# Thirty-two dense tokens of a retrieval layer take their U rows by gather; the dense U products go from 384 to 352 columns

## The chip, the core and the metric

The kernel runs on one core of a Trainium2 chip. The core has a matrix engine (TensorE, PE in the profile, with its weight loads as PEld), three elementwise engines (VectorE or DVE, ScalarE or ACT, GpSimd or POOL), a queue engine for transfers (SyncE, SP), 16 DMA engines, an on-chip memory of 128 partitions (SBUF) and accumulators (PSUM). The metric is the device time of one execution, in microseconds.

## The reference, cut to what matters

One encoder block for 512 tokens of width 1024: attention, a gated linear recurrence and their merge, and then the part that the change touches, a layer that retrieves 128 of 16384 one-neuron experts for each token (8 heads, 16 experts each):

```python
s, idx = lax.top_k(scores, K)                     # both halves of the keys, 128 each
cand = (s[:, :, 0, :, None] + s[:, :, 1, None, :]).reshape(T, PH, K * K)
cand_idx = (idx[:, :, 0, :, None] * PEER_NKEYS + idx[:, :, 1, None, :]).reshape(T, PH, K * K)
best, pos = lax.top_k(cand, K)
expert = jnp.take_along_axis(cand_idx, pos, axis=-1)
gate = jax.nn.softmax(best, axis=-1)
...
u = jnp.take(u_tab, eb, axis=0)                   # rows of U of the token's experts
a = jax.nn.gelu(jnp.einsum('td,thkd->thk', xb, u), approximate=False)
c = (a * gb).astype(h.dtype)
return jnp.einsum('thk,thkd->td', c, jnp.take(v_tab, eb, axis=0))
```

## The kernel before

The first 128 tokens (`GT`) are done by **gather**: for each of their 128 expert slots one indirect DMA on the POOL queue fetches 128 rows of a table that holds U and V side by side (1024 + 1024 numbers a row); DVE forms the dot product of the U half with the token (`rows<-rows,hrep`), ACT the activation and the gate (`gact`), and DVE adds the V half times that number to `gout`. The other 384 tokens (`ND`) are done **densely**: all 16384 experts are computed for all of them, and a matrix of gates that is zero almost everywhere picks out the right ones. The dense work goes by 128 blocks `e` of 128 experts:

- **U products** (`pieces`, `up`): for each block 8 slices of the width times 3 products (high and low parts of weights and activations, `whi`, `wlo`, `act_hi`, `act_lo`), 24 products of 128x128 weights with 384 columns. The weights are loaded (`raw<-in_u`, 3 buffers) and split by ACT (`whi`) and DVE (`wlo`). ACT's Gelu makes `gx` of the sum, and the result goes to DRAM (`gad`), or, for the last blocks (`fresh`), stays on the chip (`gf`).
- **Routing and spread** (`route`, `onehot`, `spread`): for 8 tokens `o` at a time DVE makes one-hot matrices of the two halves of the expert number (4 operations), PE multiplies them (16 products of 128 columns) into the 128x128 matrix of gates of each token, and ACT moves them to `gs`, which goes to DRAM as `gd`, 32 tokens at a time. There are 48 such steps. `fill` lets U products in between: it keeps a running sum of estimated PE time and of estimated DVE time, and issues the next slice of a U product as long as PE's sum is behind. A call `gathered(GO)` advances the gather by half a step for each `o`.
- **V stage** (`down`): for `n` = 0 to 127, in an order that mixes kept and fresh blocks, PE multiplies the weighted activations of a block with its rows of V: 3 blocks of 128 tokens, 2 halves of the width, 3 products of 512 columns, so 18 products. For that DVE weighs `ga` with the gates `gt` (`weigh`), and ACT and DVE split both operands (`chi`, `clo`, `vhi`, `vlo`). V comes by `vraw` (4 buffers), gates by `gt` (2 buffers of 4 blocks each), the kept activations by `ga` (5 buffers), all on SP's queue. The U products of fresh blocks stand between (`ups_due`), and the rest of the gather is spread evenly over the first 124 steps.

How many blocks are fresh is decided while the program is written: those that `fill` had not reached when the spread ended, less 8 (`LEAVE`) and a remainder that go before the V stage.

Of the kernel before, what the change touches and what calls it, by code (L numbers as in the profile page):

```python
# [41 lines left out]
G1, GO = 0.125, 0.5  # L42
# [10 lines left out]
ND = T - GT  # L53
GC = 0.125
# [40 lines left out]
def layout(x, positions, g_mix, w_in, g_q_lat, w_qb, g_kv_lat, w_kvb, w_a2, b_a2, g_gla, w_branch_a,  # L95
# [38 lines left out]
    a["u"] = ct(peer_u[0].reshape(128, 128, NC_D, 128).transpose(0, 3, 2, 1))  # L134
    a["uv"] = np.concatenate([peer_u[0], peer_v[0]], axis=1)
# [58 lines left out]
def body(ctx, tc, a, out):  # L194
# [209 lines left out]
    def proj(key, xs=None, bank="pmm"):  # L404
        w = weights(key)
        p = pmm(bank)
        acc(p if key[0] != "u" else p[:, GT:], pairs(w, NC_D), xs or hx)
        if key[0] != "u":
            further(key)
        return p  # L410
# [436 lines left out]
    h2d = [(hn[0][:, c, GT:], hn[1][:, c, GT:]) for c in range(NC_D)]  # L847

    def normed(c):
        q = tmp()  # L850
        dve.scalar_tensor_tensor(q[:, GT:], x2[:, c, GT:], cc(C_GFFN + c), r2[:, GT:], op0=OP.mult, op1=OP.mult)
        split(h2d[c][0], h2d[c][1], q[:, GT:], pool)
# [57 lines left out]
    aside = [columns_of] + [lambda i=i: rows_of(i) for i in range(2)] + [lambda i=i: plain_rows_of(i) for i in range(2)]  # L910
# [41 lines left out]
    gad = dr.tile([NB[0], 128, ND], F32, name="gad")  # L952

    def up_out(keep=0):

        while len(pend) > keep:
            e, p = pend.pop(0)
            if not place:
                g = tmp(n=ND)
            elif e < NB[0]:  # L960
                g = place[0].tile([128, ND], F32, name="gx", bufs=GX)
            else:
                g = ga[e] = dn.tile([128, ND], F32, name="gf", bufs=NF)
            act.activation(g, p[:, GT:], AF.Gelu)
            if e < NB[0]:
                act.dma_start(gad[e], g)
# [39 lines left out]
    sp.dma_start(gout, hd[1])  # L1006
# [3 lines left out]
    gsteps = [129]  # L1010

    def gather():

        rows = {}
# [38 lines left out]
    gd = dr.tile([128, T // TB, 128, TB], F32, name="gd")  # L1053
    GS = 2.0 ** 15
    def route(tt):
# [83 lines left out]
        if tt == 0:  # L1139
# [32 lines left out]
    def spread(o):  # L1172
# [44 lines left out]
    O0, NO = GT // 8, T // 8  # L1217
    for o in range(O0, NO + 1):
        if o < NO:
            if o == O0 or o % 16 == 0:  # L1220
# [3 lines left out]
                rate = 24.0 / (min(16, 16 - o % 16) - 1)  # L1224
            onehot(o)
# [7 lines left out]
        if o > O0:  # L1233
            spread(o - 1)
# [6 lines left out]
    EG = 4  # L1241
# [69 lines left out]
    def refill(queue=sp):  # L1311

        while made[0] < len(kept) and (made[0] < NA or kept[made[0] - NA] in used):
            e = kept[made[0]]
            ga[e] = dn.tile([128, ND], F32, name="ga", bufs=NA)
            queue.dma_start(ga[e], gad[e])
# [144 lines left out]
```

## Time and profile before

| | us |
|---|---|
| median of 3 runs (lowest to highest) | 1637.24 (1635.01 to 1640.02) |
| the profiled execution, its own time | 1637.02 |
| its span, from first to last instruction | 1635.2 |
| U, routing and spread, before the V stage (520 to 974 us) | 454 |
| V stage (974 to 1609 us) | 635 |

Read it as a list of stages: a stage is limited by its own engine or by transfers, and the mean over the span tells neither.

### The profile page before, as it was taken

Reading aid. Unit: us, or ns where it says so; the run is one execution under the profiler, and the core shown is the slowest. Engines: PE = TensorE matmul, PEld = TensorE weight load, DVE = VectorE, ACT = ScalarE, POOL = GpSimd, SP = SyncE. Lnnn points to the kernel's source line nnn. Section 1 sums busy time; section 2 is a strip of 40 time slices with the busy share of each in tenths; the row PEclk is TensorE's granted clock in tenths of the full one; section 3 lists DMA queues with packets and bytes.
Section 4 is the critical chain, followed back from the end, with each engine's and each line's share of the span. In section 5 each row is a group of like instructions: output and inputs, shape, how many; then the busy total and the mean of one; then the engine's idle time right before and its main releaser. Section 6 shows DMA issues by size and latency. Waiting matters only on the chain.

```text
span 1635.2 us, 23193 instructions
## 1 busy us (share of the span) xinstructions
PE 1603.7 (98%) x8487; PEld 1393.1 (85%) x8487; DVE 1240.3 (76%) x2517; ACT 726.0 (44%) x1252; POOL 355.6 (22%) x258
## 2 busy tenths in 40 slices
PE   7999999999999999999999999999999999999998
PEld 6777657888889999999999999888888888888876
DVE  6635665253897989889989747778988888988885
ACT  5453544243333646456455544344443443444343
POOL 4342243445354100000001111111211111111110
PEclk9999999999999999999999999999999999999999
DMA  5222122443333777788789898999999999999994
GB/s 172 64 89 78 52 71 91 169 146 110 125 115 111 233 264 279 261 311 296 266 311 348 330 345 296 318 361 347 392 383 350 386 365 370 367 344 361 364 379 152
DMA packets 154610, 415.82 MB, mean 254 GB/s; under 512 B 12343, under 2 KB 87608, under 8 KB 136448
## 3 DMA queue, kind: packets, MB, share of 16 engines
q1 hardware_dynamic: 118048, 230.28, 40.2%
q0 software_dynamic: 19888, 139.23, 22.2%
q10 hardware_dynamic: 16560, 44.83, 7.3%
q8 instruction: 66, 1.08, 0.3%
q14 instruction: 48, 0.39, 0.1%
HBM read 361.60 MB, written 52.17 MB: 253 GB/s over the span
## 4 chain that ended last, share of the span: by engine, by line
PE 83%; DMA 4%; DVE 4%; issue 4%; ACT 1%; POOL 1%; SPq 0%; DVEq 0%; POOLq 0%; ACTq 0%
PE pmm L161 61%; PE pst L161 11%; PE pk L161 10%; DMA ga<-gad 2%; DMA vraw<-in_v 1%; DVE vlo L161 1%; POOL wlo L242 1%; DMA raw<-in_u 1%; DVE rows L161 1%; DVE rB L161 0%; DVE gout L161 0%; ACT whi L236 0%; DVE tmp L161 0%; DVE clo L161 0%; DVE t L161 0%
## 5 line engine op out<-in xcount | busy, mean ns | idle before, releaser
L161 PE MATMUL pmm<-act_hi,whi 128*128 128x384 f32 (+1 forms) x1016 | 361.8, 356 | 9.4 <-ACT act_hi L331 9.0
L161 PE MATMUL pmm<-act_hi,wlo 128*128 128x384 f32 (+1 forms) x1016 | 353.5, 348 | 3.7 <-DVE wlo L161 2.0
L161 PE MATMUL pmm<-act_lo,whi 128*128 128x384 f32 (+1 forms) x1016 | 353.2, 348 | 0.5 <-DVE act_lo L161 0.5
L1019 POOL DMA_INDIRECT rows<-in_uv,gidx x128 | 130.8, 1022 | 890.5 <-DVE gout L161 846.7
L236 ACT ACTIVATE whi<-raw 128x1024 fp32r<-128x1024 f32 (+1 forms) x201 | 209.2, 1042 | 94.8 <-PE pmm L161 50.9
L242 POOL TENSOR_TENSOR wlo<-raw,whi 128x1024 fp32r<-128x1024 f32 (+1 forms) x79 | 186.2, 2361 | 250.2 <-ACT whi L236 211.5
L161 DVE TENSOR_TENSOR wlo<-raw,whi 128x1024 fp32r<-128x1024 f32 x122 | 148.9, 1223 | 91.4 <-ACT whi L236 89.8
L161 PEld LDWEIGHTS pmm<-act_hi,whi 128*128 128x128 f32 x1016 | 191.8, 189 | 23.8 <-ACT act_hi L331 9.0
L161 PEld LDWEIGHTS pmm<-act_hi,wlo 128*128 128x128 f32 x1016 | 191.6, 189 | 13.9 <-DVE wlo L161 2.6
L161 PE MATMUL pmm<-vlo,chi 128*128 128x512 f32 x512 | 200.5, 392 | 1.6 <-DVE vlo L161 1.3
L161 PE MATMUL pmm<-vhi,chi 128*128 128x512 f32 x512 | 199.6, 390 | 0.9 <-ACT vhi L1275 0.9
L161 PEld LDWEIGHTS pmm<-act_lo,whi 128*128 128x128 f32 x1016 | 192.0, 189 | 8.7 <-DVE act_lo L161 1.0
L161 PE MATMUL pmm<-vhi,clo 128*128 128x512 f32 x512 | 199.3, 389 | 0.0
L161 DVE SCALAR_TENSOR_TENSOR gout<-rows,gact,gout 128x1024 f32<-128x1024 f32 x128 | 164.4, 1284 | 0.0
L161 DVE TENSOR_TENSOR vlo<-vraw,vhi 128x1024 fp32r<-128x1024 f32 x128 | 156.4, 1222 | 4.7 <-ACT vhi L1275 4.7
L1275 ACT ACTIVATE vhi<-vraw 128x1024 fp32r<-128x1024 f32 x128 | 134.0, 1049 | 50.5 <-DMA vraw<-in_v 50.0
L161 DVE SCALAR_TENSOR_TENSOR rows<-rows,hrep 128x1024 f32<-128x1024 f32 x128 | 156.2, 1221 | 0.0
L161 PE MATMUL pmm<-t,whi 128*128 128x512 f32 x436 | 137.7, 397 | 0.0
L161 PEld LDWEIGHTS pmm<-vlo,chi 128*128 128x128 f32 x512 | 96.1, 188 | 25.7 <-DVE vlo L161 6.0
L1031 ACT ACTIVATE gact<-gact 128x1 f32<-128x1 f32 x128 | 25.8, 202 | 205.8 <-DVE rows L161 205.6
L161 PEld LDWEIGHTS pmm<-vhi,chi 128*128 128x128 f32 x512 | 96.1, 188 | 19.9 <-ACT vhi L1275 1.3
L161 PEld LDWEIGHTS pmm<-vhi,clo 128*128 128x128 f32 x512 | 96.1, 188 | 19.0
(276 smaller groups left out, 2775.3 us busy)
## 6 DMA issues: line engine op xcount, KB each, us to landing
raw<-in_u SPq DMA_DIRECT2D x128, 512.0 KB, 5.5
vraw<-in_v SPq DMA_DIRECT2D x124, 512.0 KB, 8.5
gt<-gd SPq DMA_DIRECT2D x30, 768.0 KB, 10.4
gd<-gs ACTq DMA_DIRECT2D x11, 2048.0 KB, 8.2
gad<-gx ACTq DMA_DIRECT2D x96, 192.0 KB, 5.0
ga<-gad SPq DMA_DIRECT2D x95, 192.0 KB, 9.6
raw<-in_w SPq DMA_DIRECT2D x28, 512.0 KB, 3.3
raw<-in_wpq SPq DMA_DIRECT2D x16, 512.0 KB, 3.5
```

What stands on the lines that cost most here:

```text
L161: return f(*args, **kw)
L236: act.activation(hi[:, :n], raw[:, :n], AF.Copy)
L242: (lo_eng or lo_home[0]).tensor_tensor(lo[:, :n], raw[:, :n], hi[:, :n], op=OP.subtract)
L1019: pool.indirect_dma_start(out=rows[n], out_offset=None, in_=a["uv"], in_offset=bass.IndirectOffsetOnAxis(ap=gidx[:, n:n + 1], axis=0))
L1031: act.activation(g, g, AF.Gelu)
L1275: act.activation(hi, vraw[n], AF.Copy)
```

## The change

For the first 32 of the dense tokens (`GU`, tokens 128 to 159) the U part is no longer computed densely. Their rows of U alone are gathered from a table of their own (`ur`, 1024 numbers a row; 4096 rows in 32 indirect DMAs of 128 rows each), DVE forms the dot products (`gather_u`), and the activation times the gate of each expert slot takes the place of the gate in the one-hot products. It is divided by the token's largest value, which is put into `tall`; in the V stage ACT writes `tall` into the first 32 columns of each block's activations, so that the weighing multiplies it back. The U products, Gelu and `gad` shrink to 352 columns (`GD` = 160). The four `o` steps of these tokens go to the end of the spread. The gather is advanced by 0.9 of a step for each `o`, and no longer during the first two routings. Gates lie in DRAM by groups of 4 blocks: what a `gt` load reads of one partition is one run of 6 KB, where it was 12 runs of 512 bytes, and a `gd` write puts 32 runs of 512 bytes for each partition, 1 MiB apart, where it was one run of 16 KB.

```diff
-G1, GO = 0.125, 0.5
+GO = 0.9
...
+GU = 32
+GD = GT + GU
...
-                mm3(p[:, GT:], x, y, c == 0, c == NC_D - 1)
+                mm3(p[:, GD:], x, y, c == 0, c == NC_D - 1)
...
+    def u_rows_of(i):
...
+        for c in range(4):
+            pe.matmul(ph[0:GU, c * 128:(c + 1) * 128], x2[:, 4 * i + c, GT:GD], dg[:, 4 * i + c], start=True, stop=True)
+        act.activation(hut[0][0:GU, i * 512:(i + 1) * 512], ph[0:GU], AF.Copy, scale=r2c[0:GU, 1:2])
+        if i:
+            sp.dma_start(hu, hut[0][0:GU])
...
-            act.activation(g, p[:, GT:], AF.Gelu)
+            act.activation(g[:, GU:], p[:, GD:], AF.Gelu)
             if e < NB[0]:
-                act.dma_start(gad[e], g)
+                act.dma_start(gad[e], g[:, GU:])
...
+    def gather_u():
...
+                for i in range(2):
+                    pool.indirect_dma_start(out=rows[n][:, i * D:(i + 1) * D], out_offset=None, in_=a["ur"],
+                                            in_offset=bass.IndirectOffsetOnAxis(ap=ulist[0][:, 2 * n + i:2 * n + i + 1], axis=0))
...
+        for n in range(GU // 2):
...
+            for i in range(2):
+                x = r[:, i * D:(i + 1) * D]
+                dve.scalar_tensor_tensor(x, x, 1.0, gout, op0=OP.mult, op1=OP.mult, accum_out=ulist[1][:, 2 * n + i:2 * n + i + 1])
+            fetch(n + GBUF - 1)
+            yield
...
+        dve.reduce_max(s, au, axis=AX.X)
...
+        pe.transpose(p[:, 0:GU], gu, ident[0:GU, 0:GU])
+        pe.matmul(p[:, GU:2 * GU], ones[0:GU], au[:, 0:GU], start=True, stop=True)
+        act.activation(tall, p[:, GU:2 * GU], AF.Copy)
...
-    gd = dr.tile([128, T // TB, 128, TB], F32, name="gd")
+    gd = dr.tile([128 // EG, 128, T // TB, EG * TB], F32, name="gd")
...
-            if tt:
-                gathered(G1)
...
+    turn = list(range(GD // 8, T // 8)) + list(range(GT // 8, GD // 8))
...
-            queue.dma_start(gts[n], gd[:, GT // TB:, seq[n] * EG:(seq[n] + 1) * EG, :])
+            queue.dma_start(gts[n], gd[seq[n], :, GT // TB:].rearrange("p b (j t) -> p b j t", j=EG))
...
             x3 = ga[e].rearrange("p (b t) -> p b t", t=TB)
+            act.activation(ga[e][:, :GU], tall, AF.Copy)
             dve.tensor_tensor(x3, x3, gts[n // EG][:, :, n % EG], op=OP.mult)
```

Counted in the order of PE's instructions, the 128 U blocks are divided anew: before, 24.25 of them stood ahead of the first one-hot product, 64.75 among the one-hot products, 13 between these and the V stage, and 26 inside the V stage; now it is 25.9, 85.1, 11 and 6. In the last 20 of the 48 `o` steps there stood 21 blocks, and now 32.

First place, the POOL queue from the first gather to the start of the V stage. Before (`rows` is the buffer of gathered rows, `in_uv` the table of U and V):

```order
L242 TENSOR_TENSOR wlo<-raw,whi 128x1024 x11
L1019 DMA rows<-in_uv,gidx 128x2048 x28
L1269 DMA vraw<-in_v 128x1024 x4
L1288 DMA gt<-gd 128x12x128
L1316 DMA ga<-gad 128x384 x5
L1288 DMA gt<-gd 128x12x128
L1019 DMA rows<-in_uv,gidx 128x2048 x100
```

Now (`in_ur` is the table of U alone):

```order
L245 TENSOR_TENSOR wlo<-raw,whi 128x1024 x11
L1226 DMA uidx<-pos 32x32 x4
L1041 DMA rows<-in_ur,uidx 128x1024 x32
L1058 DMA gact<-uact 32x32 x4
L1059 DMA gout<-hd 128x1024
L1088 DMA rows<-in_uv,gidx 128x2048 x24
L1353 DMA vraw<-in_v 128x1024 x4
L1372 DMA gt<-gd 128x1536
L1401 DMA ga<-gad 128x352 x5
L1372 DMA gt<-gd 128x1536
L1088 DMA rows<-in_uv,gidx 128x2048 x104
```

Ahead of the V stage 32 fetches of half the size came in and 4 of the old ones went out of it, into the V stage.

Second place, SP's queue in the first steps of the V stage, where it issues the loads of weights of fresh blocks (`raw<-in_u`) between those of V, activations and gates. Before:

```order
L1269 DMA vraw<-in_v 128x1024
L1316 DMA ga<-gad 128x384
L1269 DMA vraw<-in_v 128x1024
L223 DMA raw<-in_u 128x1024
L1288 DMA gt<-gd 128x12x128
L1269 DMA vraw<-in_v 128x1024 x2
L223 DMA raw<-in_u 128x1024
L1269 DMA vraw<-in_v 128x1024 x2
L1316 DMA ga<-gad 128x384
L223 DMA raw<-in_u 128x1024
```

Now:

```order
L1353 DMA vraw<-in_v 128x1024
L1401 DMA ga<-gad 128x352
L1353 DMA vraw<-in_v 128x1024
L1372 DMA gt<-gd 128x1536
L1353 DMA vraw<-in_v 128x1024 x4
L1401 DMA ga<-gad 128x352
L1372 DMA gt<-gd 128x1536
L1353 DMA vraw<-in_v 128x1024
L1401 DMA ga<-gad 128x352
L1353 DMA vraw<-in_v 128x1024
```

The weights of U are gone from here, since they were loaded earlier; over the V stage the loads of `ga` rise from 95 to 115 on this queue, and those of `vraw` and `gt` stay at 124 and 30.

Third place, ACT in two steps of the V stage without a U product. Before:

```order
L1031 ACTIVATE gact<-gact 128x1
L1032 ACTIVATE gact<-gact,ggat 128x1
L1301 ACTIVATE chi<-ga 128x384
L1275 ACTIVATE vhi<-vraw 128x1024
L1031 ACTIVATE gact<-gact 128x1
L1032 ACTIVATE gact<-gact,ggat 128x1
L1301 ACTIVATE chi<-ga 128x384
```

Now:

```order
L1100 ACTIVATE gact<-gact 128x1
L1101 ACTIVATE gact<-gact,ggat 128x1
L1386 ACTIVATE chi<-ga 128x384
L1359 ACTIVATE vhi<-vraw 128x1024
L1378 ACTIVATE ga<-tall 128x32
L1100 ACTIVATE gact<-gact 128x1
L1101 ACTIVATE gact<-gact,ggat 128x1
L1386 ACTIVATE chi<-ga 128x384
```

A small copy stands behind `vhi<-vraw`, and DVE's weighing of that block waits for it.

## Rows read from the trace of the kernel before

**Rows 1.** The page, part 1: busy time, share and instructions of each engine.

```profile
PE 1603.7 (98%) x8487; PEld 1393.1 (85%) x8487; DVE 1240.3 (76%) x2517; ACT 726.0 (44%) x1252; POOL 355.6 (22%) x258
```

**Rows 2.** Windows: stretch, its length, busy us by engine, clock, DMA share, GB/s.

```profile
520.00:929.00 409.00, 409.00 (x2860) 401.64 (x2859) 370.77 (x921) 214.81 (x350) 34.74 (x31) 1.00 0.79 284
974.00:1609.00 635.00, 632.54 (x2938) 540.52 (x2939) 536.55 (x710) 267.65 (x512) 99.83 (x98) 1.00 0.96 355
```

**Rows 3.** Timeline of PE: start us, us, instruction; 384 and 256 columns.

```profile
560.00 0.33 PE L161 MATMUL pmm<-act_hi,wlo 128*128 128x384 f32 x1
...
593.80 0.33 PE L161 MATMUL pmm<-act_hi,wlo 128*128 128x384 f32 x1
...
47.90 0.28 PE L161 MATMUL pk<-whi,act_hi 128*128 128x256 f32 x1
48.01 0.28 PE L161 MATMUL pk<-wlo,act_hi 128*128 128x256 f32 x1
```

**Rows 4.** The chain, 1487 to 1607 us: start us, us, what it ran through.

```profile
1487.39 2.72 PE pmm L161 x12
...
1491.47 2.72 PE pmm L161 x12
...
1502.01 16.70 DMA ga<-gad
...
1570.70 12.25 DMA ga<-gad
...
1602.47 2.72 PE pmm L161 x12
```

**Rows 5.** Timeline of PE: two sets of products for token rows.

```profile
435.29 1.05 PE L161 MATMUL pst<-t,x 128*128 128x128 f32 x8
436.18 1.06 PE L161 MATMUL pk<-t,tmp 128*128 128x128 f32 x8
```

**Rows 6.** The page, part 6: issues, size of one, median us to landing.

```profile
vraw<-in_v SPq DMA_DIRECT2D x124, 512.0 KB, 8.5
gt<-gd SPq DMA_DIRECT2D x30, 768.0 KB, 10.4
gd<-gs ACTq DMA_DIRECT2D x11, 2048.0 KB, 8.2
```

**Rows 7.** DMA from 1540 to 1580 us: total, then queues with packets, MB, share.

```profile
DMA packets 6342, 15.84 MB, mean 396 GB/s; under 512 B 381, under 2 KB 4150, under 8 KB 5289
...
q0 software_dynamic: 1183, 8.59, 53.1%
q1 hardware_dynamic: 5155, 7.21, 50.3%
```

**Rows 8.** Windows, columns as in rows 2: a longer stretch around it.

```profile
1500.00:1580.00 80.00, 78.07 (x341) 63.19 (x340) 70.47 (x96) 30.92 (x63) 15.12 (x15) 1.00 0.98 374
```

**Rows 9.** Timeline of DVE in the V stage, from one gather step on.

```profile
1200.02 1.22 DVE L161 SCALAR_TENSOR_TENSOR rows<-rows,hrep 128x1024 f32<-128x1024 f32 x1
...
1201.17 1.28 DVE L161 SCALAR_TENSOR_TENSOR gout<-rows,gact,gout 128x1024 f32<-128x1024 f32 x1
1202.36 0.55 DVE L161 TENSOR_TENSOR ga<-ga,gt 128x384 f32<-128x384 f32 x1
1202.83 0.55 DVE L161 TENSOR_TENSOR clo<-gf,chi 128x384 fp32r<-128x384 f32 x1
1203.30 1.22 DVE L161 TENSOR_TENSOR vlo<-vraw,vhi 128x1024 fp32r<-128x1024 f32 x1
1204.44 1.22 DVE L161 TENSOR_TENSOR wlo<-raw,whi 128x1024 fp32r<-128x1024 f32 x1
```

**Rows 10.** Timeline of PE: the first of 16 one-hot products, and what follows them.

```profile
899.81 0.23 PE L161 MATMUL pk<-x,xh 128*128 128x128 f16 x1
...
900.72 0.42 PE L161 MATMUL pmm<-act_hi,whi 128*128 128x384 f32 x1
```

**Rows 11.** Windows, columns as in rows 2: a busy stretch of the spread.

```profile
860.00:880.00 20.00, 20.00 (x155) 19.53 (x153) 18.26 (x26) 10.75 (x20) 2.30 (x2) 1.00 0.97 361
```

More of the change, by code (lines that the diff above doesn't have):

```diff
@@ L846, in body @@
     hn = [sb.tile([128, NC_D, T], F32R, name="act_hi"), sb.tile([128, NC_D, T], F32R, name="act_lo")]
-    h2d = [(hn[0][:, c, GT:], hn[1][:, c, GT:]) for c in range(NC_D)]
+    h2d = [(hn[0][:, c, GD:], hn[1][:, c, GD:]) for c in range(NC_D)]
     def normed(c):
         q = tmp()
-        dve.scalar_tensor_tensor(q[:, GT:], x2[:, c, GT:], cc(C_GFFN + c), r2[:, GT:], op0=OP.mult, op1=OP.mult)
-        split(h2d[c][0], h2d[c][1], q[:, GT:], pool)
+        dve.scalar_tensor_tensor(q[:, GD:], x2[:, c, GD:], cc(C_GFFN + c), r2[:, GD:], op0=OP.mult, op1=OP.mult)
+        split(h2d[c][0], h2d[c][1], q[:, GD:], pool)
     x2d = dr.tile([128, NC_D, ND], F32, name="x2d")
@@ L908, in plain_rows_of @@
             sp.dma_start(hd[1], ht[1])
-    aside = [columns_of] + [lambda i=i: rows_of(i) for i in range(2)] + [lambda i=i: plain_rows_of(i) for i in range(2)]
+    hu = dr.tile([GU, D], F32, name="hu")
+    hut = []
+    def u_rows_of(i):
+        if not i:
+            hut.append(fr.tile([128, D], F32, name="t2"))
+        ph = pmm("pst")
+        for c in range(4):
[3 more added lines that the diff above has]
+            sp.dma_start(hu, hut[0][0:GU])
+    aside = [columns_of] + [lambda i=i: rows_of(i) for i in range(2)] + [lambda i=i: plain_rows_of(i) for i in range(2)] \
+        + [lambda i=i: u_rows_of(i) for i in range(2)]
     ups = iter(range(128))
@@ L1005, in body @@
     sp.dma_start(hrep, hd[0])
-    sp.dma_start(gout, hd[1])
+    for i in range(4):
+        sp.dma_start(gout[i * GU:(i + 1) * GU], hu)
     gidx = gp.tile([128, 128], I32, name="gidx")
@@ L1009, in body, with fetch @@
     gact = gp.tile([128, 128], F32, name="gact")
-    gsteps = [129]
+    tall = gp.tile([128, GU], F32, name="tall")
+    gsteps = [GU // 2 + 129]
+    def gather_u():
+        rows = {}
+        def fetch(n):
+            if n < GU // 2:
+                rows[n] = gp.tile([128, 2 * D], F32, name="rows", bufs=GBUF)
+                for i in range(2):
+                    pool.indirect_dma_start(out=rows[n][:, i * D:(i + 1) * D], out_offset=None, in_=a["ur"],
+                                            in_offset=bass.IndirectOffsetOnAxis(ap=ulist[0][:, 2 * n + i:2 * n + i + 1], axis=0))
+        for n in range(GBUF - 1):
+            fetch(n)
+        yield
+        for n in range(GU // 2):
+            gsteps[0] -= 1
+            r = rows.pop(n)
+            for i in range(2):
+                x = r[:, i * D:(i + 1) * D]
+                dve.scalar_tensor_tensor(x, x, 1.0, gout, op0=OP.mult, op1=OP.mult, accum_out=ulist[1][:, 2 * n + i:2 * n + i + 1])
+            fetch(n + GBUF - 1)
+            yield
+        _, ua, gu, au = ulist
+        act.activation(ua, ua, AF.Gelu)
+        for i in range(4):
+            pool.dma_start(au[0:GU, i * GU:(i + 1) * GU], ua[i * GU:(i + 1) * GU])
+        pool.dma_start(gout, hd[1])
+        yield
+        yield
+        gu, au, s, rs = gu[0:GU], au[0:GU], ua[0:GU, 0:1], ua[0:GU, 1:2]
+        dve.tensor_tensor(gu, gu, au, op=OP.mult)
+        act.activation(au, gu, AF.Abs)
+        yield
+        dve.reduce_max(s, au, axis=AX.X)
+        dve.tensor_scalar(s, s, 1e-30, None, op0=OP.max)
+        dve.reciprocal(rs, s)
+        dve.tensor_scalar(gu, gu, rs, None, op0=OP.mult)
+        dve.tensor_scalar(au[:, 0:GU], ident[0:GU, 0:GU], s, None, op0=OP.mult)
+        yield
+        p = pmm()
+        pe.transpose(p[:, 0:GU], gu, ident[0:GU, 0:GU])
+        pe.matmul(p[:, GU:2 * GU], ones[0:GU], au[:, 0:GU], start=True, stop=True)
+        act.activation(tall, p[:, GU:2 * GU], AF.Copy)
+        act.activation(gh[:, 0:GU], p[:, 0:GU], AF.Copy, scale=GS)
+        dve.scalar_tensor_tensor(gl[:, 0:GU], p[:, 0:GU], GS, gh[:, 0:GU], op0=OP.mult, op1=OP.subtract)
     def gather():
+        yield from gather_u()
         rows = {}
@@ L1143, in route @@
             return
+        u = 0
+        if tt == 1:
+            u = GU
+            x, xi = (y.rearrange("p h k -> p (h k)")[0:GU] for y in (best, pos))
+            xi = xi.bitcast(I32)
+            dve.scalar_tensor_tensor(x, e1[0:GU], float(NK), e2[0:GU], op0=OP.mult, op1=OP.add)
+            dve.tensor_copy(xi, x)
+            dve.tensor_copy(ulist[2][0:GU], g.rearrange("p h k -> p (h k)")[0:GU])
+            for i in range(4):
+                pool.dma_start(ulist[0][i * GU:(i + 1) * GU], xi[:, i * GU:(i + 1) * GU])
         ts = slice(tt * 128 - GT, (tt + 1) * 128 - GT)
+        tg = slice(tt * 128 - GT + u, (tt + 1) * 128 - GT)
         p = pmm()
@@ L1212, in body @@
         for _ in route(tt):
-            if tt:
-                gathered(G1)
             fill()
     rt, due = None, 0.0
[L1217 to L1220, printed above, removed]
+    turn = list(range(GD // 8, T // 8)) + list(range(GT // 8, GD // 8))
+    for i, o in enumerate(turn + [None]):
+        if o is not None:
+            if o >= GD // 8 and (i == 0 or o % 16 == 0):
                 for _ in rt or ():
@@ L1224, in body @@
                 rate = 24.0 / (min(16, 16 - o % 16) - 1)
+            if o == GT // 8:
+                assert gsteps[0] < 128
             onehot(o)
@@ L1232, in body @@
                 fill()
-        if o > O0:
-            spread(o - 1)
+        if i:
+            spread(turn[i - 1])
         gathered(GO)
@@ L1315, in refill @@
             ga[e] = dn.tile([128, ND], F32, name="ga", bufs=NA)
-            queue.dma_start(ga[e], gad[e])
+            queue.dma_start(ga[e][:, GU:], gad[e])
             made[0] += 1
```

19 lines of the change are left out of this document (11 added, 8 removed).

## The prediction

> **What bounds the kernel now.** The page says that PE is busy for 98% of the span [rows 1], but matmuls overlap in the trace, so I read starts, not ends. In a run of U products the starts at 560.00 and 593.80 us are 195 products apart [rows 3]: 33.80 us / 195 = 173.3 ns for 384 columns, with no gap. In the V stage one step `n` of 18 products of 512 columns takes 1491.47 - 1487.39 = 4.08 us [rows 4], 226.7 ns each. So 128 columns cost 226.7 - 173.3 = 53.3 ns, or 13.3 ns for 32. Then I asked by stage whether PE waits. From 520 to 929 us it is busy all the time with the transfers (DMA) at 0.79 [rows 2]; in the V stage it is busy 632.5 of 635 us, with DMA at 0.96 [rows 2]. The reader is to see that PE sets the time in both, and that in the V stage the transfers are almost as full. The chain shows how close: from the step at 1487.39 to the one at 1602.47 there are 27 steps, which take 115.1 us where 27 x 4.08 = 110.2 would do, and the chain runs there through loads of `ga` of 16.70 and 12.25 us [rows 4]. In that stretch no U product stands between the steps. There the transfers already set the pace now and then, and cost 5 us.
>
> **The change, part by part.**
>
> *Columns.* 128 blocks x 24 products x 13.3 ns = 41.0 us less of PE. That the weight load might set a floor at 352 columns is excluded by products of 256 columns, whose starts lie 48.01 - 47.90 = 0.11 us apart [rows 3]; 352 columns should take 160.0 ns.
>
> *Added PE work.* The token rows for the gather are two sets like the one that takes 436.18 - 435.29 = 0.89 us [rows 5]: 1.8 us, and 0.3 us for a transpose and a small product. Together +2.1 us.
>
> *Where the U blocks stand.* 20 blocks leave the V stage (26 to 6) and stand before it (102 to 122). PE before the V stage: 122 x 24 x 160.0 ns - 102 x 24 x 173.3 ns = 468.5 - 424.2 = +44.3 us. V stage: 6 x 3.84 - 26 x 4.16 = -85.1 us. For PE alone that is the same -41 us as above. For the transfers it is not: the V stage gets shorter, and its loads do not.
>
> *The V stage's transfers.* For one step without U the loads are: V 0.524 MB and gates 0.197 MB (a quarter of a load) [rows 6], `ga` 128 x 352 x 4 bytes, 0.180 MB, in 112 of the last 116 steps, 0.174 MB, and rows of the gather: by the order of the instructions 105 of its steps are left for 124 V steps, 0.847 x 1.049 MB (128 x 2048 x 4 bytes) = 0.888 MB. Sum 1.783 MB. What can the queues carry? From 1540 to 1580 us they moved 396 GB/s with the two large queues at 53.1% and 50.3%, so full [rows 7]. The gather's queue q0 has pieces of 8 KB: 8.59 MB in 0.531 x 40 us is 404 GB/s. In q1 the packets of 2 to 8 KB are 6342 - 4150 - 1053 (those of q0) = 1139, V rows of 4 KB, 4.67 MB; its 2.54 MB of smaller pieces split by the packet counts into 0.92 MB of `ga` and 1.62 MB in pieces of 512 bytes, which are the gates. If V and `ga` move like q0 (13.8 us of q1's 20.1), the gates get 6.3 us, or 257 GB/s. This is what the new layout mends: 0.197 MB cost 0.77 us, and in runs of 6 KB 0.49 us. So one step costs 1.783 MB / 404 = 4.41 us of queue time; the queues ran at 103.7%, which makes 4.26 us at best. Over 80 us around it the rate was 374 and not 396 GB/s although PE was held up there [rows 8]; by that, 4.26 x 396 / 374 = 4.51 us. I take 4.45, nearer to the long stretch, since the wait in question is a long one. That is above PE's 4.08. The 6 U blocks left are used up in the first dozen steps, and loads end about 6 steps before the last, so some 110 steps run at the pace of transfers: 110 x 0.37 = 41 us, less what the buffers hold ready. The 27 steps above show that: their own loads, 1.77 MB a step, would take 121 us at 396 and 128 us at 374 GB/s, and they took 115, so 6 to 13 us were in the buffers; I take 10. So PE waits 31 us in the V stage (10 at 4.26 us, 37 at 4.51), where it waits 5 now: +26.
>
> *DVE in the V stage.* Its own pace by starts [rows 9]: 1.15 + 1.19 for a gather step, 0.47 + 0.47 for weighing and `clo`, 1.14 for `vlo`. With 0.847 gather steps this makes 1.98 + 2.08 = 4.06 us a step, as much as PE's 4.08, so it costs nothing, but it catches up on nothing either. Covered by the transfers' 4.45 us, it has 9% to spare.
>
> *The gather of U rows.* 32 operations like `rows<-rows,hrep` at 1.15 us [rows 9] are 37 us of DVE ahead of the V stage, less 4 old gather steps of 2.34 us, plus the splits of 20 more blocks at 1.14 us, as for `vlo`: +50 us, while PE's stage grows by 46. DVE was busy 371 of 409 us there [rows 2], so PE still hides it; if it does not, the excess of 4 us is the cost. Its loads of 16.8 MB go into a stage that had room, at 284 GB/s on average [rows 2].
>
> *The end of the spread.* In its last 20 steps there are now 32 U blocks, 1.6 a step: PE 1.6 x 3.84 + 0.91 (16 one-hot products, 900.72 - 899.81 [rows 10]) = 7.05 us. Loads and stores: 1.6 x (0.524 + 0.180) + 0.85 x 1.049 (17 of 20 with a gather step) + 0.524 (a quarter of a `gd` write [rows 6]) = 2.54 MB, or 360 GB/s. The busiest stretch before, 361 GB/s at 0.97, left PE without a wait [rows 11]. But now `gd` goes in pieces of 512 bytes: 2.02 MB / 404 + 0.524 / 257 = 7.04 us, just PE's time. Between nothing and 7 us (if 374 of 396 is carried), I take +5.
>
> *Small things.* The copy of `tall` is 128 short ACT operations in a stage where ACT is busy 268 of 635 us [rows 2]; hidden. If ACT were the late one, DVE's weighing would wait behind `vhi`, which waits for V (a rival below).
>
> **Sum**, against the profiled execution's own 1637.0 us: -41.0 + 2.1 + 26 + 5 = -7.9, so 1629 us. That execution is 0.2 us below the median of the runs.
>
> [...]
>
> **The rivals.**
>
> *The transfers keep up.* If the V stage carries 1.783 MB in 4.08 us (437 GB/s, above anything in the rows) or the buffers hide more, PE waits no more there at all: 1637 - 39 - 5 + 5 = 1598. For it: the long runs for the gates; against it: 396 GB/s was the top with PE already waiting [rows 4, 7]. 0.09.
>
> *The gate writes choke the spread (slower).* Each `gd` piece takes longer as a write than the gates' reads do. At twice the time of a read, 2.04 us more a step, 20 steps lose 41 us and the time is 1637 - 39 + 26 + 41 = 1665. It decides from 0.9 us a step on (18 us in all), when 0.524 MB take 2.94 instead of 2.04 us, 178 GB/s. For it: the stage is full even without it; against it: the weights are three buffers deep. [...] 0.19.
>
> *DVE and the queue's order set the V stage.* DVE has no slack of its own, and `weigh` now stands behind a copy that stands behind `vhi`; a late V row so holds up weighing too. If a step then takes 4.75 us, the wait is 110 x 0.67 - 10 = 64 us, and the time 1637 - 39 + 59 + 5 = 1662. For it: in the stretch with waits DVE was busy 70.5 of 80 us [rows 8], at a lower load. 0.10.
>
> *A lower ceiling of memory.* If over a whole stage no more than 358 GB/s are carried, one step takes 1.783 / 358 = 4.98 us, PE waits 110 x 0.90 - 10 = 89 us, and the time is 1687. Against it: 374 GB/s over 80 us [rows 8], 396 over 40. 0.04. [...]
>
> *It does not do what it says.* If 352 columns took 173 ns, 41 us are missing: 1670. The 256-column products speak against it [rows 3]. 0.02.
>
> **How the numbers follow.** My forecast has 0.56, with an own range of 1605 to 1640 (V steps from 4.26 to 4.51 us, 0 to 10 us in the spread). A measurement of this kernel tells about 0.3%, 5 us, from no change: within the forecast I put 0.34 faster, 0.18 the same, 0.04 slower. The first rival adds 0.09 to faster; the others, 0.35, go to slower but for 0.02 near the bound. So 0.43 faster, 0.20 the same, 0.37 slower. The range: 1606 leaves out most of the first rival, 1662 the far halves of the slow ones, together 0.2.
>
> **What would show it.** U products 160 ns apart; the first V product some 46 us later than now or a little more, and its steps about 4.45 us apart once the U blocks are used up, with DMA at 0.95 or more and waits for `ga`, `vraw` or `rows`; gates landing sooner. Wrong it is if the V steps stay at 4.08 us, or if PE waits in the spread for `raw` or for one-hot matrices.

## The result and the profile after

The changed kernel takes 1742.19 us (median of 4 runs, 1735.73 to 1744.31) where the kernel before takes 1637.12 beside it: 1.0637 times as long (95% interval 1.0614 to 1.066). The forecast was 1629 us, in a range of 1606 to 1662. It is wrong in sign and outside its range.

Two stages hold the whole difference. I read the start of each V step, that is of its first product with `vhi`, in both traces, and set the terms of the forecast beside them:

| | before | forecast | after |
|---|---|---|---|
| first V step starts | 986.1 | 1037.5 (+44.3 +2.1 +5) | 1079.6 |
| first to last V step | 637.9 | 578.8 (-85.1 +26) | 642.9 |
| last V step to the end | 11.2 | 11.2 | 11.4 |

So 42 us went astray before the V stage and 64 in it; 1629 + 42 + 64 is 1735, the time of the profiled execution (1735.73, the fastest of the four). First the page, part 1: busy us, share and instructions of each engine (to [rows 1]):

```profile
PE 1624.4 (94%) x8506; PEld 1364.9 (79%) x8506; DVE 1285.2 (74%) x2591; ACT 734.4 (42%) x1386; POOL 390.5 (23%) x299
```

And windows of the two stages, with the columns of [rows 2]:

```profile
520.00:1033.00 513.00, 490.54 (x3422) 478.80 (x3421) 425.71 (x1014) 242.96 (x390) 75.28 (x68) 0.97 0.83 278
1079.00:1709.00 630.00, 575.51 (x2400) 439.47 (x2399) 522.61 (x695) 246.16 (x595) 96.28 (x102) 1.00 0.95 349
```

PE no longer fills either stage. It idles 22 us ahead of the V stage, where it idled nowhere, and at least 54 us in it; no engine is busy in the V window for more than 575 of 630 us, and the transfers move 349 GB/s, less than before. That is the sign of a chain that runs through several engines, not of one that is full. Only the share of the DMA engines, 0.95, is as high as it was, so transfers stay a rival (theory B below).

**The V stage.** Next, one V step of the changed kernel in the timeline of DVE (start us, us, instruction, and in brackets the idle time before it and what ended it).

```profile
1312.72 1.22 DVE L164 SCALAR_TENSOR_TENSOR rows<-rows,hrep 128x1024 f32<-128x1024 f32 x1
...
1313.86 1.28 DVE L164 SCALAR_TENSOR_TENSOR gout<-rows,gact,gout 128x1024 f32<-128x1024 f32 x1
1316.02 0.56 DVE L164 TENSOR_TENSOR ga<-ga,gt 128x384 f32<-128x384 f32 x1 [0.88 <-ACT ga L1378]
1316.50 0.55 DVE L164 TENSOR_TENSOR clo<-ga,chi 128x384 fp32r<-128x384 f32 x1
1316.96 1.24 DVE L164 TENSOR_TENSOR vlo<-vraw,vhi 128x1024 fp32r<-128x1024 f32 x1
1318.13 1.21 DVE L164 SCALAR_TENSOR_TENSOR rows<-rows,hrep 128x1024 f32<-128x1024 f32 x1
```

The same step in the timeline of ACT:

```profile
1313.97 0.20 ACT L1100 ACTIVATE gact<-gact 128x1 f32<-128x1 f32 x1 [3.37 <-DVE rows L164]
1314.21 0.29 ACT L1101 ACTIVATE gact<-gact,ggat 128x1 f32<-128x1 f32 x1
1314.41 0.51 ACT L1386 ACTIVATE chi<-ga 128x384 fp32r<-128x384 f32 x1
1314.83 1.04 ACT L1359 ACTIVATE vhi<-vraw 128x1024 fp32r<-128x1024 f32 x1
1315.77 0.21 ACT L1378 ACTIVATE ga<-tall 128x32 f32<-128x32 f32 x1
```

Read it as a circle. DVE's dot product (1312.72) releases ACT's Gelu `gact` (1313.97, 1.25 us on). Behind that in ACT's queue stand `chi` and `vhi`, and behind these the copy of `tall`; it releases DVE's weighing at 1316.02, 2.05 us on. Weighing, `clo` and `vlo` take DVE to its next dot product at 1318.13, 2.11 us on. The circle is 5.41 us long, although DVE idles 0.88 us in it and ACT waits 3.37 us before it. PE's step is 4.08 us. Before, DVE's weighing needed nothing new from ACT, and no circle was closed. The groups of waits from 1079 to 1709 us (who waited for whom: us in total, times, longest) show how often:

```profile
...
ACT gact L1100 <- DVE rows L164: 355.6, 105, 3.8
DVE ga L164 <- ACT ga L1378: 89.9, 98, 2.4
...
PE pmm L164 <- DVE vlo L164: 48.5, 79, 0.7
```

ACT waits for DVE in all 105 steps with a gather, DVE waits for the copy 98 times, and PE for DVE's last operand. Of the 122 steps without a U product 64 take 5.3 to 5.6 us, and the mean of all 122 is 4.92. No transfer is among the large waits (`ga` has 1.6 us in total). V rows and gates land sooner than in [rows 6], as the page's part 6 says (KB of one, median us to landing):

```profile
vraw<-in_v SPq DMA_DIRECT2D x124, 512.0 KB, 6.4
gt<-gd SPq DMA_DIRECT2D x30, 768.0 KB, 8.1
gd<-gs ACTq DMA_DIRECT2D x11, 2048.0 KB, 14.9
```

**The spread.** The third of these lines is the other place: a write of `gd` lands after 14.9 us, where it took 8.2. ACT's timeline behind one of them (ACTq is ACT's own issuing of transfers):

```profile
859.67 0.38 ACTq L1275 DMA_DIRECT2D gd<-gs  x1
...
862.83 9.73 ACTq L984 DMA_DIRECT2D gad<-gx  x1
872.65 1.06 ACT L239 ACTIVATE whi<-raw 128x1024 fp32r<-128x1024 f32 x1 [9.86 <-issue]
```

The write itself is issued in 0.38 us. The next transfer on that queue, a small one, takes 9.73 us to issue, and ACT does nothing in that time: the split `whi` of the next weights, which PE needs, starts 9.86 us after ACT's last work. In the kernel before, ACT's timeline has both at 0.33 us:

```profile
868.08 0.33 ACTq L1191 DMA_DIRECT2D gd<-gs  x1
...
872.99 0.33 ACTq L966 DMA_DIRECT2D gad<-gx  x1
```

Each of the eleven whole writes is followed by such a long issue, and of the last write, which goes in four parts one right after the other, three are such; these 14 issues take 88 us together. The first ones cost PE little. Behind five of the later ones it waits 3.2 to 5.3 us each, 28.1 us in all from 520 to 1080 us with the short waits, and its clock falls. PE's timeline has its first product after one gap:

```profile
873.76 0.66 PE L164 MATMUL pmm<-act_hi,whi 128*128 128x352 f32 x1 [5.32 <-ACT whi L239]
```

Three windows around it, with the columns of [rows 2], so the granted clock is the third number from the end:

```profile
864.00:868.00 4.00, 4.00 (x37) 3.86 (x36) 0.00 (x0) 0.00 (x0) 0.29 (x1) 1.00 1.11 371
868.00:874.00 6.00, 0.68 (x4) 0.39 (x3) 0.26 (x1) 1.34 (x2) 0.00 (x0) 0.82 0.91 318
874.00:879.00 5.00, 3.70 (x20) 2.80 (x21) 4.97 (x7) 2.82 (x6) 0.00 (x0) 0.50 0.61 198
```

After 5.3 us without work the clock granted to TensorE is 0.50, that is 1.2 GHz, in the next stretch. There are five such stretches, of 3 to 10 us, between 870 and 1046 us, one at each gap. PE is busy for 28.3 us in them, at half the clock, which costs another 14.2 us, so a gap costs more than its length.

**The columns** came near what they should (to [rows 3]). PE's timeline in the unbroken run of U products, and in two runs that follow each other in the spread:

```profile
560.00 0.33 PE L164 MATMUL pmm<-act_hi,wlo 128*128 128x352 f32 x1
...
592.50 0.33 PE L164 MATMUL pmm<-act_hi,wlo 128*128 128x352 f32 x1
...
631.07 0.33 PE L164 MATMUL pmm<-act_hi,wlo 128*128 128x352 f32 x1
...
640.57 0.32 PE L164 MATMUL pmm<-act_hi,wlo 128*128 128x352 f32 x1
...
641.88 0.32 PE L164 MATMUL pmm<-act_lo,whi 128*128 128x352 f32 x1
...
650.58 0.32 PE L164 MATMUL pmm<-act_hi,wlo 128*128 128x352 f32 x1
```

195 products in 32.50 us are 166.7 ns, 57 in 9.50 us are 166.7 ns, 55 in 8.70 us are 158.2 ns; 160.0 was forecast, from 173.3. A run of U products keeps one pace or the other: of the 42 unbroken runs of 30 products or more, 31 lie at 158.2 to 158.6 ns, 10 at 166.5 to 166.7, and one goes over from the first to the second in its middle. Without the pauses the mean of all U products is 161.4 ns.

### The profile page after: what moved, and what is told of

It reads as the page before. It is cut to its first block, busy times and chain, and to the rows that moved or that the text cites. A ratio compares the mean times of both kernels' runs of the same rounds, so it can differ in the third digit from the quotient of the medians.

```text
span 1734.0 us, 23597 instructions
## 1 busy us (share of the span) xinstructions
PE 1624.4 (94%) x8506; PEld 1364.9 (79%) x8506; DVE 1285.2 (74%) x2591; ACT 734.4 (42%) x1386; POOL 390.5 (23%) x299
## 5 line engine op out<-in xcount | busy, mean ns | idle before, releaser
L164 PE MATMUL pmm<-act_hi,whi 128*128 128x352 f32 (+1 forms) x1176 | 409.8, 349 | 30.4 <-ACT whi L239 21.2
L164 PE MATMUL pmm<-act_hi,wlo 128*128 128x352 f32 (+1 forms) x1176 | 401.6, 342 | 6.0 <-DVE wlo L164 4.3
L164 PE MATMUL pmm<-act_lo,whi 128*128 128x352 f32 (+1 forms) x1176 | 400.1, 340 | 0.5 <-DVE act_lo L164 0.5
L1088 POOL DMA_INDIRECT rows<-in_uv,gidx x128 | 123.2, 962 | 719.7 <-DVE gout L164 709.8
L164 PEld LDWEIGHTS pmm<-act_hi,whi 128*128 128x128 f32 x1176 | 225.5, 192 | 46.8 <-ACT whi L239 23.8
L164 PE MATMUL pmm<-vlo,chi 128*128 128x512 f32 x512 | 208.7, 408 | 48.5 <-DVE vlo L164 48.5
L164 PEld LDWEIGHTS pmm<-act_hi,wlo 128*128 128x128 f32 x1176 | 224.7, 191 | 19.0 <-DVE wlo L164 7.9
L164 PEld LDWEIGHTS pmm<-act_lo,whi 128*128 128x128 f32 x1176 | 225.5, 192 | 8.7 <-DVE act_lo L164 1.0
L164 PE MATMUL pmm<-vhi,clo 128*128 128x512 f32 x512 | 207.3, 405 | 6.0 <-DVE clo L164 0.3
L164 DVE TENSOR_TENSOR ga<-ga,gt 128x384 f32<-128x384 f32 x120 | 66.8, 559 | 99.9 <-ACT ga L1378 89.9
L1359 ACT ACTIVATE vhi<-vraw 128x1024 fp32r<-128x1024 f32 x128 | 133.4, 1044 | 4.9 <-DMA vraw<-in_v 4.3
## 6 DMA issues: line engine op xcount, KB each, us to landing
gd<-gs ACTq DMA_DIRECT2D x11, 2048.0 KB, 14.9
```

The lines of the kernel that those rows point to most:

```text
L164: return f(*args, **kw)
L1359: act.activation(hi, vraw[n], AF.Copy)
```

## The experiments

**Theory A**: ACT sets both stages, in the V stage by the place of the copy of `tall`, in the spread because a write of 4096 pieces fills its queue. **Theory B**: transfers set both stages, since the gather of U rows adds 16.8 MB to a program that was nearly full. Twelve kernels ran, of which one measures products by themselves. In the table, ratios are to runs of the kernel before on the same chip, "V starts" and "V lasts" are the first V step's start and first to last step, and numbers are those of the experiments below.

| kernel | us | ratio to before (95%) | V starts | V lasts |
|---|---|---|---|---|
| the changed one | 1742.2 | 1.064 (1.061 to 1.066) | 1079.6 | 642.9 |
| 1: copy of `tall` a step early | 1697.4 | 1.038 (1.035 to 1.041) | 1083.3 | 598.3 |
| 2: old layout of `gd` | 1709.2 | 1.045 (1.042 to 1.048) | 1050.0 | 647.8 |
| 3: early copy, `gd` in four parts | 1653.3 | 1.010 (1.007 to 1.013) | 1044.1 | 598.1 |
| 4: early copy, old layout | 1682.0 | 1.030 (1.027 to 1.033) | 1043.2 | 619.2 |
| 5: before, with the new layout | 1665.2 | 1.019 (1.016 to 1.021) | 1020.0 | 632.0 |
| 6: before, new layout in four parts | 1636.6 | 1.001 (0.999 to 1.002) | 991.4 | 632.0 |
| 7: as 3, half of each gathered row | 1601.4 | 0.980 (0.978 to 0.982) | 1041.3 | 547.2 |
| 8: as 3, 18 U blocks in V | 1621.6 | 0.989 (0.987 to 0.991) | 1003.3 | 607.6 |
| 9: as 3, 26 U blocks in V | 1636.4 | 0.999 (0.997 to 1.001) | 997.6 | 630.3 |
| 11: as 3, sums from PSUM column 0 | 1654.5 | 1.009 (1.007 to 1.012) | 1045.8 | 596.5 |
| 12: 8 and 11 together | 1622.8 | 0.991 (0.988 to 0.993) | 1009.4 | 601.8 |

**1. The copy of `tall` one step earlier**, ahead of `chi` and `vhi`; the same number of copies. `tall_in` issues the copy for a block that is on its way, once; the other blocks get theirs where they had it.

```diff
     for n in range(128 - ENDS):
         down(n)
+        tall_in(n + 5)
         c_hi(n + 3)
         v_hi(n + 3)
```

> The changed kernel with one move: ACT's copy of tall for a block is issued one V step earlier, ahead of the chi and vhi of that step, so DVE's weighing finds it done. The 128 copies are all still there. Theory A (the copy behind vhi closes a loop between DVE and ACT: rows, gact, chi, vhi, tall, weigh, clo, vlo, rows, 5.4 us a step): steps with a gather fall from 5.39 to 4.1 to 4.5 us, the V stage gets about 60 us shorter, the time is about 1675. Theory B (the transfers set the V stage's pace, their share is 0.95 to 0.99): steps stay at 5 us on the mean, the time stays at 1736.

The V stage gives back 44.6 us, of some 60 expected, with the copies all still there; so it was their place, not their work. DVE's timeline has weighing without a wait:

```profile
1313.48 0.55 DVE L164 TENSOR_TENSOR ga<-ga,gt 128x384 f32<-128x384 f32 x1
```

ACT's timeline in the same step:

```profile
1312.83 0.21 ACT L1379 ACTIVATE ga<-tall 128x32 f32<-128x32 f32 x1
1312.95 0.51 ACT L1393 ACTIVATE chi<-ga 128x384 fp32r<-128x384 f32 x1
1313.37 1.05 ACT L1359 ACTIVATE vhi<-vraw 128x1024 fp32r<-128x1024 f32 x1
```

Weighing starts at 1313.48 behind DVE's own work, while ACT is still at `vhi`. The spread is as slow as it was.

**2. The old layout of `gd`** in the changed kernel, with the write and the load that belong to it, nothing else.

```diff
-    gd = dr.tile([128 // EG, 128, T // TB, EG * TB], F32, name="gd")
+    gd = dr.tile([128, T // TB, 128, TB], F32, name="gd")
...
```

> The changed kernel with the old layout of the gates in DRAM: one run of 16 KB a partition for a gd write, 12 runs of 512 bytes for a gt load. Theory A (a gd write of 4096 pieces fills ACT's queue, the next gad issue waits 4 to 10 us on ACT, and PE waits for whi): no issue on ACT over 1.5 us, the V stage starts about 40 us earlier, at some 1040 us, and stays as long as it is now, time about 1695. Theory B (the spread is full because of bytes): the bytes are the same, so the spread gains at most 10 us, and the V stage loses up to 30 by its gates in small pieces: 1730 to 1755.

No issue takes over 1 us any more, and the V stage starts 29.6 us earlier, where 40 were expected; 69 of its steps still take 5.3 to 5.6 us. The same pair of transfers as above in ACT's timeline, a write, then `gad`:

```profile
880.73 0.33 ACTq L1275 DMA_DIRECT2D gd<-gs  x1
882.02 0.33 ACTq L984 DMA_DIRECT2D gad<-gx  x1
```

**3. The early copy, and each `gd` write in four parts** of 1024 pieces, one after each of the next `o` steps.

```diff
...
+            gpend.extend([lambda i=i: part(i) for i in range(parts)])
+            gpend.pop(0)()
+            while tb == GT // TB and gpend:
+                gpend.pop(0)()
```

> The changed kernel with the early copy of tall and with each gd write cut into 4 writes of 1024 pieces, one after each of the next o steps. Theory A: no long issue on ACT, V steps of 4.1 to 4.5 us, time 1625 to 1640, about that of the kernel before. Theory B: above 1690.

89 us of the 105 lost are back, and the layout's gain for the gates' loads is kept; at 1653 it is 13 us above the range of theory A. Against the first experiment the V stage starts 39.2 us earlier. Six issues still take over 1 us, 18 us in all, three of them at the last write, whose parts still go one right after the other.

**4. The early copy with the old layout.**

> The changed kernel with the early copy of tall and the old layout of the gates. Theory A: the spread as in the run with the old layout alone; in the V stage the gates in pieces of 512 bytes cost some 0.28 us a step of transfer time on top, 4.4 to 4.7 us a step: 1630 to 1660. If the new layout is worth nothing in the V stage, as fast as the run with the writes in parts, or faster. Theory B: above 1690.

At 1682 it lies above theory A's range and below theory B's. Its V stage is 21.1 us longer than that of the third experiment, where only the layout of the gates differs: with the circle gone, transfers show. (The profiled execution is the fastest of its four; by the medians the two kernels are 28.8 us apart.) Both theories have a part, A the larger.

**5 and 6. The layout alone, in the kernel before**: whole writes, and in four parts as in the third experiment. Of the first, the write:

```diff
...
-                act.dma_start(gd[:, tb, i * n:(i + 1) * n].rearrange("p i t -> p (i t)"),
-                              gs[:, i * n:(i + 1) * n].rearrange("p i t -> p (i t)"))
+                act.dma_start(gd[i * n // EG:(i + 1) * n // EG, :, tb].rearrange("g p x -> p g x"),
+                              gs[:, i * n:(i + 1) * n].rearrange("p (g j) t -> p g (j t)", j=EG))
```

> The kernel before with the new layout of gd alone: writes in one piece of work each (4096 pieces of 512 bytes), loads of gt in runs of 6 KB; all tokens' U products stay at 384 columns. If ACT's queue blocks on such a write whatever else the kernel does (theory A), the transfer that ACT issues next after each write takes some 4 to 10 us to issue, as in the changed kernel (14 issues, 83 us over the usual 0.33), the V stage starts some 15 to 35 us later than before (there are fewer U products among the one-hot steps to run dry, but DVE's and ACT's work stands behind it all the same), and the V stage gets at most its 5 us of waits back: 1645 to 1670. If the block came of the fuller transfers of the changed kernel (theory B: the DMA engines were busy with U rows), the issues stay near 0.33 us here, since transfers run at 0.79 in this stage, and the time is 1630 to 1638.

> The kernel before with the new layout of gd, and each write cut into four (1024 pieces each), one after each of the next o steps. Theory A: no long issue on ACT's queue, no later start of the V stage (within 3 us), and the gates' loads in long runs give back some of the 5 us for which PE waits in the V stage: 1630 to 1637. Theory B, by which 512-byte writes load the DMA engines themselves: the pieces cost the same whether in one write or in four, so this kernel comes out as slow as the one with whole writes.

Whole writes cost 33.9 us ahead of the V stage without any gather of U rows, so the block doesn't need the change's fuller transfers. In four parts the pieces are as many and the bytes the same, and no issue takes over 1.9 us: it is the number of pieces given out at once that blocks, not their size or place. ACT's timeline in the kernel with whole writes:

```profile
862.26 0.41 ACTq L1192 DMA_DIRECT2D gd<-gs  x1
863.24 7.53 ACTq L966 DMA_DIRECT2D gad<-gx  x1
```

And in the one with parts:

```profile
862.58 0.38 ACTq L1196 DMA_DIRECT2D gd<-gs  x1
864.03 0.34 ACTq L966 DMA_DIRECT2D gad<-gx  x1
```

The V stage gives back 5.9 us in both, PE's waits there. But in parts the V stage also starts 5.3 us later, 2 more than I allowed, and the time is that of before.

**7. Half of each gathered row.** The third experiment's kernel, where a fetch for the 128 gathered tokens brings 1024 numbers and not 2048. It leaves out their V rows: DVE's second operation works on the same half as its first.

```diff
-                pool.indirect_dma_start(out=rows[n], out_offset=None, in_=a["uv"],
+                pool.indirect_dma_start(out=rows[n][:, :D], out_offset=None, in_=a["ur"],
```

> The changed kernel with tall copied a step early and gd written in four parts (1653 us), where each fetch of the 128 gathered tokens brings 1024 numbers a row and not 2048, that is 0.5 MB and not 1 MB; the V half of those rows is left out, DVE does the same operations on the half that came, so the result for the first 128 tokens isn't the reference's. Nothing else on any engine changes. If transfers are what is left in the V stage (theory B for the rest), a step's loads fall from 1.78 to 1.34 MB, 3.4 us of queue time, and PE sets the pace again: steps of 4.1 us, V stage 545 to 560 us (it was 598), time 1595 to 1612. If DVE's work or the order of its queue is what is left (theory A for the rest), steps stay at 4.5 to 4.6 us and the time at 1645 to 1655.

All engines do what they did, and the V stage falls from 598.1 to 547.2 us, which is PE's own work (637.9 - 5 - 85.1 = 547.8). So what was left there was transfers. Windows of the third experiment, its V stage and the full stretch in it:

```profile
1044.00:1642.00 598.00, 572.82 (x2480) 463.10 (x2479) 518.79 (x707) 254.50 (x607) 102.69 (x102) 0.97 0.95 368
...
1236.00:1585.00 349.00, 330.37 (x1370) 260.26 (x1369) 313.72 (x426) 147.76 (x360) 66.49 (x67) 0.97 1.00 394
```

The V stage's window in this one:

```profile
1041.00:1588.00 547.00, 546.98 (x2480) 456.86 (x2479) 516.71 (x706) 253.17 (x607) 103.82 (x102) 1.00 0.87 303
```

And the third experiment's waits for transfers, from 1044 to 1642 us (us, times, longest):

```profile
DVE ga L164 <- DMA ga<-gad: 49.0, 20, 5.7
ACT vhi L1368 <- DMA vraw<-in_v: 27.8, 21, 4.1
```

The V stage starts only 2.8 us earlier, although 24 of the lighter fetches stand ahead of it: the spread was hardly held up by transfers.

**8 and 9. Fewer U blocks ahead of the V stage.** The third experiment leaves 6 U blocks for a V stage that waits for transfers, and each block made earlier goes to `gad` and back. A factor on DVE's sum in `fill` leaves more: 0.93 leaves 18, 0.87 leaves 26.

```diff
-        while left[0] and pe.ns - begun[0] < dve.ns - begun[1]:
+        while left[0] and pe.ns - begun[0] < 0.93 * (dve.ns - begun[1]):
```

> The changed kernel with tall copied a step early and gd written in four parts (1653 us), and with the planner that lets U products in between the one-hot steps held to 0.93 of DVE's sum: 75.25 U blocks stand among the one-hot products (85.1), and 18 in the V stage (6). Twelve blocks fewer are written to gad and read again (0.36 MB a block, 4.3 MB), and their PE work of 46 us goes from a stage where PE waits for nothing into one where PE waits for transfers. If transfers are what is left (theory B for the rest), the spread gets some 40 us shorter, the V stage goes from 598 to some 605 us (PE's own work there 591), and the time is 1610 to 1630, at or below that of the kernel before. Rival: DVE, busy 425 of the 476 us from 520 to 996, sets the spread once PE has less to do; then it gets at most 25 us shorter, the V stage grows by 20 or more, and the time is 1640 to 1655.

> The same with 0.87: 67.4 U blocks among the one-hot products and 26 in the V stage, as in the kernel before. Theory B for the rest: the spread some 60 us shorter than 380 us, unless DVE, which would be busy about 403 of some 410 us there, holds it up by more; the V stage 622 us of PE work and 603 us of transfers at 392 GB/s, so 630 us; time 1618 to 1635. Rival (DVE sets the spread): 1640 or more, and more than the kernel with 18 blocks.

18 blocks come out as forecast: the spread, from its first to its last one-hot product, is 37.6 us shorter, the V stage 9.5 longer, the time 1621.6 us, faster than both kernels. Thirteen issues of ACT still take over 1 us there, 30 us together, but up to the end of the spread PE waits only 4 us. With 26 blocks the spread gets 56 us shorter and the V stage lasts the 630 us expected, but the time is 1636.4, between the two theories: in the stretch to the end of the spread DVE is busy 395.2 us of 416, and PE waits 20 us there, each time for an instruction of DVE. The window of that stretch with 18 blocks:

```profile
520.00:953.00 433.00, 428.72 (x3134) 420.71 (x3133) 410.08 (x1000) 225.40 (x366) 74.64 (x68) 1.00 0.89 308
```

And with 26:

```profile
520.00:936.00 416.00, 395.88 (x2899) 385.13 (x2898) 395.16 (x989) 211.45 (x342) 76.69 (x68) 0.99 0.87 301
```

**10 to 12. The columns.** Products by themselves, 192 in a row for each case, and then the one placement that came out shorter, in the kernel, alone and with 18 blocks.

```diff
-                mm3(p[:, GD:], x, y, c == 0, c == NC_D - 1)
+                mm3(p[:, :T - GD], x, y, c == 0, c == NC_D - 1)
```

> Computes none of the layer (its output is a copy of x): 192 products in a row for each of twelve cases of columns and of the place of the first column in the moving operand and in PSUM: 512, 384, 352 (columns 160 on, as in the changed kernel), 352 from column 128, 352 from column 0, 352 with PSUM from column 0, 368, 336, 320, 256, and 384 and 352 once more. If a product takes as long as its columns say, on the line through 512 at 226.7 and 384 at 173.3 ns (0.417 ns a column), 352 take 160.0, 368 take 166.7, 336 take 153.3 and 320 take 146.7 ns, wherever the columns stand. If the place matters (the first column is no multiple of 64 or 128), 352 from 160 on take 166.7 ns as in the changed kernel's unbroken run, and 160.0 from column 0 or 128. If a step in the number of columns matters, all of 352 take 166.7.

> The changed kernel with tall copied a step early and gd in four parts (1653 us), where the U products are summed in columns 0 to 351 of PSUM and no longer in columns 160 to 511; the moving operand still begins at column 160. In the measurement of products by themselves that went from 167.0 to 158.4 ns. If the place in PSUM is what makes 352 columns slow, the unbroken run of U products from 525 to 600 us has starts 158 to 161 ns apart (it was 166.7), the V stage starts 4 to 10 us earlier, and the time is 1643 to 1650. If not, starts stay at 166.7 ns and the time at 1650 to 1656.

> Both: sums in PSUM from column 0 on, and 18 U blocks left for the V stage. If the two add up: 4 to 10 us less than with 18 blocks alone, 1603 to 1625. If transfers set the pace in both stages by then, the shorter products give less than 3 us more.

In the kernel of products ACT reads each case's sum when its last product ends, so in ACT's timeline the starts of these reads are 192 products apart:

```profile
91.20 0.49 ACT L46 ACTIVATE o<-p 128x384 f32<-128x384 f32 x1 [32.71 <-PE p L44]
123.27 0.47 ACT L46 ACTIVATE o<-p 128x352 f32<-128x352 f32 x1 [31.57 <-PE p L44]
154.19 0.47 ACT L46 ACTIVATE o<-p 128x352 f32<-128x352 f32 x1 [30.46 <-PE p L44]
185.12 0.46 ACT L46 ACTIVATE o<-p 128x352 f32<-128x352 f32 x1 [30.47 <-PE p L44]
215.53 0.47 ACT L46 ACTIVATE o<-p 128x352 f32<-128x352 f32 x1 [29.95 <-PE p L44]
```

Of 352 columns, the kernel's placement (column 160 of the activations and of PSUM) takes 32.07 / 192 = 167.0 ns, columns from 128 and from 0 take 161, and column 160 of the activations with PSUM from column 0 takes 158.4. None of the three rules expected gives all four. And in the kernel the last placement changed nothing: its unbroken run still has 195 products in 592.45 - 559.95 = 32.50 us, 166.7 ns, and the kernels with it are at 1654.5 and 1622.8 us, as without it. Of the 45 unbroken runs in experiment 11's trace 34 lie near 158.3 ns and 11 near 166.6, much as in the changed kernel. So the placement doesn't choose between these two paces, and the products by themselves, one run for each case but the kernel's own and each behind another case, couldn't show it. What chooses stays open.

## Why the prediction was wrong, by its steps

**Columns, -41.0: held, 4 us too large.** The U products follow each other at 161.4 ns on the mean, where the trace of before has 173.4: 128 x 24 of them save 37 us.

**"The copy of `tall` is 128 short ACT operations in a stage where ACT is busy 268 of 635 us [rows 2]; hidden": this step failed, 45 us.** A busy share says that an engine has time, not when. The text named the way out ("weighing would wait behind `vhi`") and looked for its trigger in V rows that come late. The trigger was already in the trace of before and needed nothing late: ACT's queue holds `gact`, which waits for DVE's dot product, so whatever stands behind it waits for DVE too, and DVE's weighing stands behind that. Summed with DVE's times of [rows 9] and the distances of ACT's starts above, the circle is 1.15 + 0.24 + 0.20 + 0.42 + 0.94 + 0.25 + 0.47 + 0.47 + 1.14 = 5.28 us, against PE's 4.08. The rival "DVE and the queue's order set the V stage" was the right one for this stage, at 0.10, but it too needed a late V row, and the waits from 1079 to 1709 us have none for `vraw`; its 4.75 us a step was a guess, near the 4.92 measured on the mean.

**"The end of the spread", +5: failed, 36 of the 42 us** (1079.6 - 1044.1, by the third experiment; 39 by the first against the third, 30 by the second). The sum had the bytes of the `gd` pieces and their time on the DMA engines. It had nothing for the engine that issues them: 4096 pieces held up ACT's next transfer by 4 to 10 us, and ACT splits PE's weights. PE's trace accounts for it: without the +5 the V stage would have started at 1032.5, 47.1 us earlier, and 28.1 us of waits, 14.2 us for the low clock and 4.4 us for products at 161.5 instead of 160.0 ns (122 x 24) make 46.7. The rival "the gate writes choke the spread" had the place and nearly the price (41 us), but by another mechanism, a piece that takes twice as long. That part didn't happen: from 859 to 873 us, behind one such write, the queues of the DMA engines show for q10, ACT's,

```profile
q10 hardware_dynamic: 3839, 1.97, 47.3%
```

(packets, MB, share of 16 engines), that is 0.473 x 16 x 14 us / 3839 = 27.6 ns for 512 bytes, or 297 GB/s if a queue had all engines. That is no slower than the 257 GB/s which the prediction worked out for reads of such pieces. The Trainium skill's "DMA: Bandwidth & Descriptors", section Latency and other measured facts, gives 164 GB/s for copies between tensors in memory whose rows lie 2 MiB apart, where 214 is full. No run here makes such copies, and these writes, 1 MiB apart, show no such loss.

**"The V stage's transfers", +26: right in kind, too small by 19 us.** Without the circle the V stage lasts 598.1 us and without half of the rows 547.2, so transfers cost some 50 us where 31 were forecast. The bytes were right: in the third experiment's full stretch 76 steps take 349 us, 4.59 us each, at 394 GB/s, 1.81 MB a step (1.783). The rate taken, 1.783 MB in 4.45 us or 401 GB/s, was above what a long stretch carries. The first 20 steps after the last U block run at 4.08 us from the buffers, as said; after that steps of 4.1 and 4.4 us are broken by ten single ones of 6 to 11 us, and in six of these the granted clock is 0.5 for 3 to 7 us.

**"DVE ... costs nothing" ahead of the V stage: held** where PE had its blocks: DVE was busy 425 of 476 us in the third experiment.

**What the change is worth.** With both stalls mended it is still 1.0% slower than before: some 37 us of PE are bought with transfers, and the V stage then waits for transfers. The planner had also filled the spread with U blocks, 20 more of which went to DRAM and back, 0.36 MB each. Leaving 12 of them for the V stage, where PE has time, makes it 1.1% faster than before. Whether the kernel before would gain by the same factor wasn't tried.

## What to carry to other kernels

Before costing an operation at nothing because its engine is half idle, write down what stands ahead of it in that engine's queue and what each of those waits for; if the engine that waits for the new operation is among them, add up the whole circle and hold it against the step. Count the pieces of a DMA as work of the engine that issues it and of everything behind it there, and give the pieces out in parts between other work. And when work is taken off the full engine by adding transfers, move some of that engine's work to the stage where it waits for them, as long as no other engine then sets the stage it came from.

## What was not expected of the hardware

- A write of 4096 pieces of 512 bytes is issued in 0.38 us, but the next transfer of the same engine took 3 to 11 us to issue instead of 0.33, in all three kernels that had such writes whole; once, in the fifth experiment, it took 0.95 us, when it came 6.6 us after the write. Parts of 1024 pieces mostly passed in 0.38 us; with the DMA engines full (share 1.00 from 800 to 996 us in the third experiment) single issues still took up to 7.8 us, and up to 8.2 in the kernels with 18 blocks.
- Products of 352 columns with the same placement ran at 158.2 to 158.6 ns in 31 unbroken runs of the changed kernel and at 166.5 to 166.7 in 10, at full clock in both; by themselves they took 158.4, 161.0 and 167.0 ns, in one or two runs each. 384 columns took 173.3 and 256 took 120.0.
